# A hybrid encoder layer: gate tiles first, seven products for every q, k and v block, and attention pairs of two groups in turn

## The chip, the cores and the metric

The kernel runs on one core of one Trainium2 chip, in float32: products are built from pairs of rounded float32 (`float32r`) parts, a high and a low one. The metric is device microseconds of one execution; each kernel is timed in several executions, and one execution is profiled. Engines are named as in the profile: PE is TensorE, PEld its weight loads, DVE VectorE, ACT ScalarE, POOL GpSimd, SP SyncE, whose queue issues all the DMAs of this kernel.

## What is computed

The input x has 512 positions (a grid of 8 rows by 64 columns) of 2048 values. One projection gives q, k, v and a gate for two groups of 16 heads of 64 values:

```
h = einsum('bsd,de->bse', x, w_in)                     # 2048 -> 8192
qa, ka, va, ga, qb, kb, vb, gb = split(h)              # 1024 columns each
ya = dilated_attention(qa, ka, va, t5_bias)            # group A, all 512 keys under a mask
yb = neighbourhood_attention(qb, kb, vb, na_rpb)       # group B, 8 rows x 16 columns of keys
y  = concat(ya * silu(ga), yb * silu(gb))
x  = layer_norm(alpha * x + y @ w_out)
```

Group A merges three dilated windows by their softmax denominators, which is one softmax over all keys with a bias that holds mask, bucket bias and multiplicity. Group B has a learned bias by row and column distance.

## The kernel before

**Products in parts.** Every factor is split into a high part (ACT copies it to `float32r`) and a low part (DVE subtracts), `split`, L81 to L83. A product takes three matmuls: high x high, low x high, high x low.

**Stages.** They follow each other on PE:

1. `plain_block` (L219) computes v of group A directly: 16 slices of the contraction, 8 accumulators of 128 x 512 in all eight PSUM banks, three matmuls for each, 384 in all. While it runs, ACT and DVE split x and build the sums of its quarters that the next stage needs (`combine`, L277).
2. `strassen_block` (L292) computes each of the five other q, k and v blocks from quarters, with seven products instead of eight (p1, p5, p7, p6, p3, p2, p4 in this order). A product takes 48 matmuls of 512 columns (v) or 96 of 256 (q, k). Weights come in tiles `braw` of 512 KB; DVE adds two tiles (L332) ahead of four of the products. Results are stored to DRAM by `store_v` and `store_kq`, high and low parts side by side.
3. Between blocks, `prep_a` (L130, after k of group A) builds group A's bias: a small float32 product of 33 rows by 16 columns (L139), 16 row DMAs to `rows_d`, and 8 DMAs that spread them to `biasa_d`. `prep_b` (L147, after q of A and k of B) builds group B's: 17 loads into `rpbs`, three DVE tables `gt`, 24 DMAs to `biasb_d`, rows of 1152.
4. The attention stage (L572 to L597) is one loop of 132 steps; a step is a quarter of a head's queries (128), and 32 heads in pairs make 128. Pairs 0 to 7 are group A, 8 to 15 group B. Step n issues on PE: the scores of step n (two matmuls, L465 and L466 or L473 and L474), the transposes of step n - 3 (L486), at every fourth step the product with v of the head before (L506), and between them fillers (`fill`), which are matmuls of other work. The order of PE in this loop is that of the program. The fillers are first the 16 gate tiles (`gate_unit`, L392, 48 matmuls each, two weight units of 512 KB), then half of the output projection for all four column blocks (`out_first`, L541, 384 matmuls); `amount` (L577) says how many a step takes.
5. A score step goes PE (`sc`), DVE (L437: adds the bias, takes the minimum), ACT (L439: exponent and its sum), DVE (L441: reciprocal), ACT or DVE (scaling), PE (transpose `pt`), ACT (`th`, L492), DVE (`tl`, L493), and after four steps PE with v, then ACT and DVE (L513 to L521) for the gated result `yk`.
6. The rest of the output projection (384 matmuls) and the layer norm.

**Loads of a pair.** `load_pair` (L406) loads one pair ahead: q in two DMAs of 256 KB, high parts on partitions 0 to 63 and low parts on 64 to 127; k in four DMAs of 256 KB, each head's high and low rows on both partition halves; v in four DMAs. The scores multiply the stacked q (128 rows) with k's high part and then with k's low part. Gate results stay in SBUF (`sgs`).

**What sets the order.** Outside the attention loop on PE, a scheduler places the instructions of each engine by its own estimate. ACT, DVE and the queue of SP work strictly in that order; a DMA whose tile is not free yet holds up all DMAs behind it on SP.

Of the kernel before, what the change touches and what calls it, by code (L numbers as in the profile page):

```python
# [12 lines left out]
D = 2048  # L13
# [49 lines left out]
BLOCKS = (("v", 0), ("v", 1), ("k", 0), ("q", 0), ("k", 1), ("q", 1))  # L63


def hybrid_layer(tc, xT, xn, w_in, w_gate, w_out, t5x, brow, rpb, cmask, eye, gain, lbias, out):
    nc = tc.nc
    from contextlib import ExitStack
    with ExitStack() as ctx:
# [38 lines left out]
        def load_split(ring, src, name="w"):  # L108
            raw = ring.next(name + "raw")
            nc.sync.dma_start(raw[:, :1024], src)  # L110
            h, l = halves.next(name + "h", F32R), halves.next(name + "l", F32R)
            split(raw[:, :1024], h, l)
            return h, l
# [12 lines left out]
        bias_d = dram.tile([H, 128, 560], F32, name="biasa_d"), dram.tile([H, 128, 1152], F32, name="biasb_d")  # L126
        kq_d = {(kind, g): dram.tile([PAIRS, 128, 2, S], F32, name=f"{kind}{g}_d") for kind in "kq" for g in range(2)}
        v_d = [dram.tile([S, D], F32, name=f"v{g}_d") for g in range(2)]

        def prep_a():  # L130
            nc.sync.dma_start(ident, eye)
            bt = ring_b.next("bias")
            t5 = bt[0:33, 1024:1040]
            nc.sync.dma_start(bt[0:33, :ROW], brow)
            nc.sync.dma_start(t5, t5x)
            row = ring_b.next("bias")
            for i in range(2):
                ps = bank(pss, "sc")
                nc.tensor.matmul(ps[0:16], t5, bt[0:33, 512 * i:512 * i + 512], start=True, stop=True)  # L139
                nc.scalar.activation(row[0:16, 512 * i:512 * i + 512], ps[0:16], AF.Copy)  # L140
            for c in range(16):
                nc.sync.dma_start(rows_d[:, c], row[0:16, :ROW])
            for r in range(8):
                nc.sync.dma_start(bias_d[0][:, 16 * r:16 * r + 16],
                                  _view(rows_d, 463 - 64 * r, [[16 * ROW, 16], [ROW - 1, 16], [1, 560]]))

        def prep_b(g):  # L147
            b0 = slot("b0", F32, "rpbs")
            r = b0[:, :720].rearrange("p (d j) -> p d j", d=15)
            masks = b0[:, 720:864].rearrange("p (v j) -> p v j", v=3)  # L150
            nc.sync.dma_start(masks, cmask)
            for c in range(16):
                nc.sync.dma_start(r[8 * c:8 * c + 8],
                                  _view(rpb, PADB + 8 * g * RPB - 1 + c * (RPBW - 1), [[RPB, 8], [31, 15], [1, 48]]))
            for v in range(3):
                gt = slot("b1", F32, "gt")[:, :720].rearrange("p (d j) -> p d j", d=15)
                w = 32 if v == 0 else 48
                o = 16 if v == 0 else 0
                nc.vector.tensor_tensor(gt[:, :, 0:w], masks[:, v:v + 1, 0:w].to_broadcast([128, 15, w]),
                                        r[:, :, o:o + w], ALU.subtract)  # L160
                if w < 48:
                    nc.vector.tensor_copy(gt[:, :, w:], masks[:, v:v + 1, w:].to_broadcast([128, 15, 48 - w]))
                gt = gt.rearrange("p d j -> p (d j)")
                for k in range(8):
                    nc.sync.dma_start(_view(bias_d[1], (1024 * g + 16 * k) * 1152 + 384 * v,
                                            [[1152, 16], [128 * 1152, 8], [1, 384]]),
                                      gt[:, 48 * (7 - k):48 * (7 - k) + 384])
# [51 lines left out]
        def plain_block(src, g):  # L219
            ring = Ring("r8", "r9", "t4", "t5", "t6", "t7")  # L220
            sums = Ring("t0", "t1", "t2", "t3")
            accs = [[bank(pacc, "acc") for _ in range(4)],
                    [bank(pss, "sc"), bank(pss, "sc"), bank(pst, "pt"), bank(pst, "pt")]]

            def mms(n, k, w, ch, t):
                h, l = X[k][:, 0, 128 * t:128 * t + 128], X[k][:, 1, 128 * t:128 * t + 128]
                cols = slice(512 * ch, 512 * ch + 512)
                acc = accs[ch][t]
                nc.tensor.matmul(acc, h, w[0][:, cols], start=n == 0, stop=False)  # L229
                nc.tensor.matmul(acc, l, w[0][:, cols], start=False, stop=False)  # L230
                nc.tensor.matmul(acc, h, w[1][:, cols], start=False, stop=n == 15)  # L231

            pending, raws, last = None, [], []
            for i in range(8):
                xr = slot(f"r{i}", F32, "xraw")[:, :1024].rearrange("p (s q) -> p s q", s=2)
                raws.append(xr)
                for s in range(2):
                    k, n = i + 8 * s, 2 * i + s
                    if n == 0:
                        raw = ring.next("wraw")  # L240
                        w = halves.next("wh", F32R), halves.next("wl", F32R)

                        def xpart(c):
                            nc.sync.dma_start(xr[:, 0, c], xT[0][:, c])
                            split(xr[:, 0, c], X[0][:, 0, c], X[0][:, 1, c])
# [5 lines left out]
                        xpart(slice(0, 128))  # L251
                        wpart(slice(0, 512))
                        xpart(slice(128, 512))
                        wpart(slice(512, 1024))
                    else:
                        nc.sync.dma_start(xr[:, s], xT[n])
                        split(xr[:, s], X[k][:, 0], X[k][:, 1])
                        w = load_split(ring, src[n])
                    if n < 14:
                        for ch in range(2):  # L260
                            for t in range(4):
                                mms(n, k, w, ch, t)
# [4 lines left out]
            for ch in (1, 0):  # L267
                for t in range(4):
                    for n, k, w in last:
                        mms(n, k, w, ch, t)  # L270
            for t in range(4):
                store("v", g, 1, t // 2, t % 2, accs[1][t])
            combine(7, raws[7], sums)
            for t in range(4):
                store("v", g, 0, t // 2, t % 2, accs[0][t])
# [16 lines left out]
        def strassen_block(src, kind, g):  # L292
# [9 lines left out]
            def product(i, pool, tiles, pre=None):  # L302
                accs = [bank(pool, "acc") for _ in range(2)]
                for u in range(4):
# [4 lines left out]
                    for t in range(2):  # L309
                        for kk in range(2):  # L310
# [11 lines left out]
                            for n in range(2):  # L322
# [4 lines left out]
                                nc.tensor.matmul(o, l[:, c], ah, start=False, stop=k == 7 and n == 1)  # L327
                return accs
# [58 lines left out]
        units = iter(range(32))  # L387
        raw_ring, sg_ring = Ring("r8", "r9"), Ring(*(f"n{i}" for i in range(6, 12)))
# [3 lines left out]
        def gate_unit():  # L392
# [8 lines left out]
            sg = sg_ring.next("sg")  # L401
            nc.scalar.activation(sg, acc, AF.Tanh, scale=0.5)
            nc.vector.scalar_tensor_tensor(sg, sg, 1.0, acc, op0=ALU.add, op1=ALU.mult)
            sgs.append(sg.rearrange(orders[0], b=4, r=8))

        def load_pair(i):  # L406

            g, j = divmod(i, PAIRS)
            t0 = 4 * (i % 2)
            qt = slot(f"t{t0 + 3}", F32R, "q").rearrange("p (a n) -> p a n", a=2)  # L410
            at = 128 * 2 * S * j
            for s in range(2):
                nc.sync.dma_start(f(qt[64 * s:64 * s + 64]),
                                  _view(kq_d["q", g], at + S * s, [[2 * S, 64], [128 * S, 2], [1, S]]))
            qs = [qt[:, a].rearrange("p (b n) -> p b n", b=4) for a in range(2)]
            ks = []
            for a in range(2):
                kt = slot(f"t{t0 + a}", F32R, f"k{a}")
                for d in range(2):
                    nc.sync.dma_start(f(kt[64 * d:64 * d + 64]),  # L420
                                      _view(kq_d["k", g], at + 128 * S * a, [[2 * S, 64], [1, 2 * S]]))
                ks.append(kt.rearrange("p (s n) -> p s n", s=2))
# [3 lines left out]
            return qs, ks, vv.rearrange("p b (h e) -> p b h e", h=2)  # L426
# [23 lines left out]

        def load_bias(h):
            bias = ring_b.next("bias")
            hg = h % 16
            n = 560 if h < 16 else 1152
            nc.sync.dma_start(bias[:, :n], bias_d[h // 16][hg])
            biases[h] = bias

        def scores(n):

            h, b = divmod(n, 4)  # L460
            qs, ks, _ = loaded[h // 2]
# [267 lines left out]
```

## Time and profile before

| what | value |
|---|---|
| three runs | 1017.04, 1021.34 (median), 1022.0 us |
| the profiled execution | 1018.34 us |
| its span (first to last instruction) | 1016.6 us |
| PE, DVE, ACT busy | 98%, 74%, 51% of the span |
| mean granted clock of PE | 0.992 |
| bytes moved | 189.55 MB, mean 186 GB/s |
| plain block, from its first matmul | 5.1 to 92.8 us |
| v of group B | 92.8 to 168.9 us |
| k and q of both groups | 168.9 to 500.6 us |
| attention with fillers, first score to last product with v | 511.5 to 942.6 us |
| last matmul | 1005.2 us |

A row of the timeline has start, length, engine, line, operation, output and inputs, and in brackets how long the engine had waited and for whom; a matmul also shows the rows and columns of the array that it uses. A row of the waits has total, number and longest. A row of the groups has count, busy time, mean in ns, and the idle time ahead. Matmuls are pipelined: each is shown with its modelled end, so that rows overlap, and the pace is read from start to start.

### The profile page before, as it was taken

How to read it: one execution, taken by the hardware profiler on the slowest of the kernel's cores; microseconds unless marked ns; L12 is line 12 of the kernel's file. 1: busy time of each engine (PE TensorE's matmuls, PEld its weight loads, DVE VectorE, ACT ScalarE, POOL GpSimd, SP SyncE). 2: the span in 40 equal slices, each digit the busy share in tenths (PEclk: the TensorE clock that was granted, in tenths of full speed). 3: DMA queues.
4: the chain of work that ended last, by engine and by line, in shares of the span. 5: the costliest groups of instructions: out<-in, count | busy, mean ns of one | idle time of the engine just before them, and what ended most of it. 6: DMA issues, size and time to landing. Idle time of an engine off the chain costs nothing.

```text
span 1016.6 us, 15728 instructions
## 1 busy us (share of the span) xinstructions
PE 992.3 (98%) x5901; PEld 875.3 (86%) x5901; DVE 753.4 (74%) x1257; ACT 520.2 (51%) x862; POOL 13.3 (1%) x13
## 2 busy tenths in 40 slices
PE   9999999999989999999999999999999899999995
PEld 7888888999989999999978888888888788888884
DVE  8826988887858878888657777777766577666677
ACT  7514444444424534454457777777666555556300
POOL 0000000000000000000000000000000000000022
PEclk9999999999989999999999999999999999999998
DMA  9923356347989889535865665655679997545112
GB/s 343 322 88 127 122 162 239 97 132 248 207 230 268 230 250 309 190 125 144 212 201 147 166 166 147 167 167 159 192 207 262 284 213 210 181 132 182 62 63 103
DMA packets 114675, 189.55 MB, mean 186 GB/s; under 512 B 46087, under 2 KB 70279, under 8 KB 114600
## 3 DMA queue, kind: packets, MB, share of 16 engines
q1 hardware_dynamic: 114600, 188.56, 62.4%
q8 instruction: 46, 0.75, 0.3%
q14 instruction: 29, 0.24, 0.1%
HBM read 148.67 MB, written 44.43 MB: 190 GB/s over the span
## 4 chain that ended last, share of the span: by engine, by line
PE 88%; DMA 5%; DVE 3%; SPq 1%; ACT 1%; issue 1%; POOL 0%; DVEq 0%; ACTq 0%; POOLq 0%
PE acc L398 14%; PE acc L537 14%; PE acc L327 9%; PE acc L325 9%; PE acc L326 9%; PE pv L506 5%; PE pt L486 4%; PE acc L319 3%; PE acc L318 2%; PE acc L320 2%; PE acc L229 1%; PE acc L230 1%; PE acc L231 1%; PE sc L466 1%; PE sc L465 1%; DMA wraw<-in_w_gate 1%
## 5 line engine op out<-in xcount | busy, mean ns | idle before, releaser
L82 ACT ACTIVATE wh<-braw 128x1024 fp32r<-128x1024 f32 x140 | 148.5, 1062 | 205.4 <-PE acc L326 151.4
L83 DVE TENSOR_TENSOR wl<-braw,wh 128x1024 fp32r<-128x1024 f32 x140 | 170.5, 1222 | 51.9 <-ACT wh L82 51.9
L325 PE MATMUL acc<-xk,wh 128*128 128x256 f32 x512 | 143.4, 282 | 1.1 <-ACT wh L82 1.1
L326 PE MATMUL acc<-xk,wh 128*128 128x256 f32 x512 | 143.1, 281 | 0.0
L398 PE MATMUL acc<-xk,wh 128*128 128x512 f32 x512 | 142.6, 402 | 0.0
L327 PE MATMUL acc<-xk,wl 128*128 128x256 f32 x512 | 140.6, 281 | 0.0
L83 DVE TENSOR_TENSOR wl<-wraw,wh 128x1024 fp32r<-128x1024 f32 (+1 forms) x73 | 88.1, 1207 | 46.5 <-ACT wh L82 43.2
L439 ACT ACTIVATE p<-s,mn 128x512 f32<-128x512 f32 (+2 forms) x128 | 82.0, 641 | 59.1 <-DVE mn L437 57.6
L327 PE MATMUL acc<-op,wl 128*128 128x256 f32 x384 | 106.4, 286 | 5.2 <-DVE wl L83 5.2
L325 PE MATMUL acc<-op,wh 128*128 128x256 f32 x384 | 108.4, 285 | 0.0
L326 PE MATMUL acc<-op,wh 128*128 128x256 f32 x384 | 108.4, 285 | 0.0
L537 PE MATMUL acc<-wh,yk 128*128 128x512 f32 x320 | 106.5, 401 | 0.0
L82 ACT ACTIVATE wh<-wraw 128x1024 fp32r<-128x1024 f32 (+1 forms) x73 | 76.4, 1046 | 57.0 <-PE pt L230 16.6
L398 PEld LDWEIGHTS acc<-xk,wh 128*128 128x128 f32 x512 | 91.2, 188 | 15.5
L332 DVE TENSOR_TENSOR braw<-braw 128x1024 f32<-128x1024 f32 x80 | 96.6, 1221 | 6.3 <-DMA braw<-in_w_in 5.6
L325 PEld LDWEIGHTS acc<-xk,wh 128*128 128x128 f32 x512 | 97.3, 190 | 2.4 <-ACT wh L82 1.5
L326 PEld LDWEIGHTS acc<-xk,wh 128*128 128x128 f32 x512 | 97.3, 190 | 0.0
L327 PEld LDWEIGHTS acc<-xk,wl 128*128 128x128 f32 x512 | 95.9, 190 | 0.0
L492 ACT ACTIVATE th<-pt 128x512 fp32r<-128x512 f32 (+2 forms) x128 | 65.5, 513 | 42.2 <-PE pt L486 40.6
L493 DVE TENSOR_TENSOR tl<-pt,th 128x512 fp32r<-128x512 f32 (+2 forms) x128 | 75.0, 587 | 15.2 <-ACT th L492 14.1
L327 PEld LDWEIGHTS acc<-op,wl 128*128 128x128 f32 x384 | 72.9, 194 | 5.8 <-DVE wl L83 5.8
L325 PEld LDWEIGHTS acc<-op,wh 128*128 128x128 f32 x384 | 74.3, 193 | 0.0
(157 smaller groups left out, 1840.1 us busy)
## 6 DMA issues: line engine op xcount, KB each, us to landing
braw<-in_w_in SPq DMA_DIRECT2D x80, 512.0 KB
wraw<-in_w_gate SPq DMA_DIRECT2D x32, 512.0 KB
k<-k_d SPq DMA_DIRECT2D x64, 256.0 KB
wraw<-in_w_out SPq DMA_DIRECT2D x32, 512.0 KB
biasb_d<-gt SPq DMA_DIRECT2D x48, 192.0 KB
bias<-biasb_d SPq DMA_DIRECT2D x16, 576.0 KB
v_d<-vst SPq DMA_DIRECT2D x16, 512.0 KB
k_d<-kst SPq DMA_DIRECT2D x32, 256.0 KB
```

Source lines behind the costliest of these rows:

```text
L82: nc.scalar.activation(hi, raw, AF.Copy)
L83: nc.vector.tensor_tensor(lo, raw, f(hi), ALU.subtract)
L325: nc.tensor.matmul(o, h[:, c], ah, start=k == 0 and n == 0, stop=False)
L326: nc.tensor.matmul(o, h[:, c], al, start=False, stop=False)
L327: nc.tensor.matmul(o, l[:, c], ah, start=False, stop=k == 7 and n == 1)
L332: nc.vector.tensor_tensor(dst[u], dst[u], other[u], ALU.add)
L398: nc.tensor.matmul(acc, w[:, k * 128:k * 128 + 128], X[8 * u + k][:, s], start=u == 0 and n == 0 and k == 0, stop=u == 1 and n == 2 and k ...
L439: nc.scalar.activation(p[:, :n].rearrange("p (b r c) -> p b r c", r=8, c=16), s[:, :n].rearrange(order, r=8, c=16), AF.Exp, bias=mn, scale ...
L492: nc.scalar.activation(th, pt[:, :nch], AF.Copy)
L493: nc.vector.tensor_tensor(tl, pt[:, :nch], f(th), ALU.subtract)
L506: nc.tensor.matmul(pv[:, q0:q1], vv[:, kc, a], src[:, 128 * s:128 * s + q1 - q0], start=m == 0 and n == 0, stop=m == 1 and n == 3)
L537: nc.tensor.matmul(acc, yk[k][:, s, c], w[:, wk], start=first and kk == 0 and n == 0, stop=last and kk == 1 and n == 2)
```

## The change

- **Opening.** `plain_block` now computes six gate tiles (`EARLY`) instead of v of group A: weights `w_early` of 768 columns a slice, gates as the rows of the result, six accumulators, 288 matmuls (the first slice does two tiles in halves). The gated values go to DRAM (`sg_d`).
- **Blocks.** All six q, k, v blocks go through `strassen_block`, v of group A first.
- **Bias tables.** `prep_a` and `prep_b` return lists of steps, and `strassen_block` runs one after each product (`hooks`): A's during v of group B, B's during k of A and k of B. Group B's rows shrink from 1152 to 896 elements.
- **Attention.** Pairs alternate: A, B, A, B (`ORDER`). Ten gate tiles are left as fillers; all gate results go through `sg_d`, and `load_pair` loads one. `amount` is 6.75 fillers a step on average in the first 64 steps and 5.75 after.
- **Scores.** k is loaded once, in four DMAs of 128 KB, with high and low parts on the two partition halves; q's high part twice (two DMAs of 256 KB) and its low part once (256 KB). The first score matmul multiplies the doubled high part of q (128 rows) with both parts of k, the second q's low part with k's high part, on 64 partitions (`me`).

```diff
+ORDER = [(m % 2, m // 2) for m in range(2 * PAIRS)]
+EARLY = 6
+BIAS = ((0, 32), (256, 48), (640, 32))
+BW = 896
...
-        def plain_block(src, g):
+        def plain_block(src):
...
-            accs = [[bank(pacc, "acc") for _ in range(4)],
-                    [bank(pss, "sc"), bank(pss, "sc"), bank(pst, "pt"), bank(pst, "pt")]]
+            accs = [bank(p, "acc") for p in (pacc, pacc, pacc, pacc, pss, pss)]
+            width = 128 * EARLY
...
+            for j in (4, 5, 0, 1, 2, 3):
+                for n, k, w in last:
+                    mms(n, k, w, j)
+                sg = (vst.next("sg"), 512 * (j % 2))
+                o = sg[0][:, sg[1]:sg[1] + 512]
+                silu(o, accs[j])
+                nc.sync.dma_start(sg_d[j], o)
...
+                next(hooks, lambda: None)()
                 return accs
...
-        plain_block(w_in[0:16], 0)
-        for i, (kind, g) in enumerate(BLOCKS[1:], 1):
-            strassen_block(w_in[16 * i:16 * i + 16], kind, g)
-            if i == 2:
-                prep_a()
-            elif i in (3, 4):
-                prep_b(i - 3)
+        plain_block(w_early)
+        hooks = {1: prep_a(), 2: prep_b(0), 4: prep_b(1)}
+        for i, (kind, g) in enumerate(BLOCKS):
+            strassen_block(w_in[16 * i:16 * i + 16], kind, g, iter(hooks.get(i, ())))
...
+            sg = sg_ring.next("sg")
+            nc.sync.dma_start(sg, sg_d[i])
...
+            for d in range(2):
+                nc.sync.dma_start(f(qt[64 * d:64 * d + 64]), _view(kq_d["q", g], at, [[2 * S, 64], [128 * S, 2], [1, S]]))
+                nc.sync.dma_start(f(kt[64 * d:64 * d + 64, 0]), _view(kq_d["k", g], at + S * d, [[2 * S, 64], [1, S]]))
+            nc.sync.dma_start(f(ql), _view(kq_d["q", g], at + S, [[2 * S, 128], [1, S]]))
+            for d in range(2):
+                nc.sync.dma_start(f(kt[64 * d:64 * d + 64, 1]),
+                                  _view(kq_d["k", g], at + 128 * S + S * (1 - d), [[2 * S, 64], [1, S]]))
...
+            me, cols = slice(64 * a, 64 * a + 64), slice(128 * b, 128 * b + 128)
             sc = bank(pss, "sc")
-            if h < 16:
-                nc.tensor.matmul(sc, q, kh, start=True, stop=False)
-                nc.tensor.matmul(sc, q, kl, start=False, stop=True)
...
+            o, ko = sc, (kt[:, a], kt[me, a])
...
+            for k, (m, q) in enumerate(zip(ko, (qt[:, a, cols], ql[me, cols]))):
+                nc.tensor.matmul(o, q, m, start=k == 0, stop=k == 1)
...
-            for _ in range(16):
-                yield from gate_unit()
+            for j in range(EARLY, 2 * PAIRS):
+                yield from gate_unit(j)
...
-                amount = 8 if n < 64 else 9 if n < 88 else 11
+                amount = (7, 6, 7, 7)[n % 4] if n < 64 else (6, 5, 6, 6)[n % 4]
```

The first place is SP's queue at the bias tables. `braw` are weight tiles of the blocks, `rpbs` the rows of group B's bias, `rows_d` and `biasa_d` group A's rows and their spread form, `k_d` and `v_d` stored results. Before, behind the last tile of the third weight quarter of q of group A:

```order
L298 DMA braw<-in_w_in 128x1024
L151 DMA rpbs<-in_cmask 128x144
L153 DMA rpbs<-in_rpb 8x15x48
L142 DMA rows_d<-bias 16x1024 x5
L207 DMA k_d<-kst 256x1x256 x4
L142 DMA rows_d<-bias 16x1024 x11
L153 DMA rpbs<-in_rpb 8x15x48 x2
L144 DMA biasa_d<-rows_d 16x16x560 x8
L153 DMA rpbs<-in_rpb 8x15x48 x5
L298 DMA braw<-in_w_in 128x1024
```

Now, during v of group B:

```order
L330 DMA braw<-in_w_in 128x1024
L216 DMA v_d<-vst 128x1024 x2
L167 DMA rpbs<-in_cmask 128x144
L169 DMA rpbs<-in_rpb 8x15x48
L149 DMA rows_d<-bias 16x1024 x16
L330 DMA braw<-in_w_in 128x1024 x2
L153 DMA biasa_d<-rows_d 16x16x560 x6
L330 DMA braw<-in_w_in 128x1024 x2
L153 DMA biasa_d<-rows_d 16x16x560 x2
L169 DMA rpbs<-in_rpb 8x15x48 x10
L330 DMA braw<-in_w_in 128x1024
```

Before, 33 table DMAs stand between one weight tile and the next; now 18, then 6, then 12.

The second place is PE at the ninth score step, the first of the second pair (`sc` scores, `k` and `q` the pair's tiles, `acc` and `wh` a gate tile and its weights, `pt` a transpose). Before:

```order
L465 MATMUL sc<-k_5409,q 128x512
L466 MATMUL sc<-k_5409,q 128x512
L398 MATMUL acc<-xk_99,wl 128x512
L398 MATMUL acc<-xk_100,wl 128x512
L398 MATMUL acc<-xk_101,wl 128x512
L398 MATMUL acc<-xk_102,wl 128x512
L486 MATMUL pt<-ident,p 128x128 x4
```

Now:

```order
L507 MATMUL sc<-k,q 128x256
L507 MATMUL sc<-k,ql 128x256
L428 MATMUL acc<-xk_106,wh 128x512
L428 MATMUL acc<-xk_107,wh 128x512
L428 MATMUL acc<-xk_100,wh 128x512
L521 MATMUL pt<-ident,p 128x128 x4
```

The second pair is now of group B, with 256 key columns at its first step, three fillers stand ahead of the transposes instead of four, and the second score matmul reads `ql`.

More of the change, by code (lines that the diff above doesn't have):

```diff
@@ L130, in prep_a @@
         def prep_a():
[L131 to L140, printed above, removed]
@@ new lines, in rows @@
+            def rows():
+                nc.sync.dma_start(ident, eye)
+                bt = ring_b.next("bias")
+                t5 = bt[0:33, 1024:1040]
+                nc.sync.dma_start(bt[0:33, :ROW], brow)
+                nc.sync.dma_start(t5, t5x)
+                row = ring_b.next("bias")
+                for i in range(2):
+                    ps = bank(pss, "sc")
+                    nc.tensor.matmul(ps[0:16], t5, bt[0:33, 512 * i:512 * i + 512], start=True, stop=True)
+                    nc.scalar.activation(row[0:16, 512 * i:512 * i + 512], ps[0:16], AF.Copy)
+                for c in range(16):
+                    nc.sync.dma_start(rows_d[:, c], row[0:16, :ROW])
@@ L500, in values @@
         def values(h):
[L501 to L502 removed]
+            g, i, a, _ = head(h)
+            vv = loaded[i][1]
             pv = bank(pst, "pv")
[L504 removed]
+            for m, (src, parts) in enumerate(zip(turned.pop(h), (opening, whole) if g else (full, full))):
                 for n, (kc, q0, q1, s) in enumerate(parts):
@@ L708 @@
         "w_in": wi,
+        "w_early": we,
         "w_gate": wg,
```

208 lines of the change are left out of this document (103 added, 105 removed).

## The prediction

> **What bounds the kernel now.** I read the head of the page first, then the time by stage.
>
> ```profile
> span 1016.6 us, 15728 instructions
> PE 992.3 (98%) x5901; PEld 875.3 (86%) x5901; DVE 753.4 (74%) x1257; ACT 520.2 (51%) x862; POOL 13.3 (1%) x13
> PE   9999999999989999999999999999999899999995
> PEclk9999999999989999999999999999999999999998
> PE 88%; DMA 5%; DVE 3%; SPq 1%; ACT 1%; issue 1%; POOL 0%; DVEq 0%; ACTq 0%; POOLq 0%
> ```
>
> TensorE (PE) is busy for 98% of the span and makes up 88% of the chain that ended last. It dips in two of the 40 slices, at about 280 and 785 us. So the time is the number of matmuls times their pace, plus what PE loses at a few places. Next the busy times in stretches that I cut at the stage borders (the first matmuls of each source line): plain block, v block, the four k and q blocks in three pieces, the first gate tile, group A, group B in three pieces, end of the output projection, tail. Columns: PE, weight loads, VectorE (DVE), ScalarE (ACT), GpSimd, granted clock, DMA share, GB/s.
>
> ```profile
> 5.10:92.80 87.70, 87.70 (x386) 72.62 (x386) 56.56 (x104) 40.25 (x70) 0.00 (x0) 1.00 0.64 233
> 92.80:168.90 76.10, 76.10 (x337) 63.05 (x336) 66.05 (x68) 36.33 (x42) 0.00 (x0) 1.00 0.55 180
> 264.30:320.00 55.70, 50.50 (x403) 49.89 (x402) 38.46 (x41) 19.18 (x21) 0.00 (x0) 0.94 0.85 237
> 320.00:500.60 180.60, 179.49 (x1510) 179.08 (x1509) 148.44 (x159) 82.68 (x95) 0.00 (x0) 1.00 0.72 213
> 500.60:511.50 10.90, 10.90 (x50) 9.01 (x49) 4.71 (x6) 4.68 (x5) 0.00 (x0) 1.00 0.78 209
> 511.50:714.00 202.50, 201.55 (x1004) 166.06 (x1003) 151.72 (x346) 144.32 (x275) 0.00 (x0) 1.00 0.60 165
> 714.00:780.00 66.00, 66.00 (x350) 56.06 (x349) 46.81 (x123) 43.77 (x98) 0.00 (x0) 1.00 0.76 207
> 780.00:803.00 23.00, 19.63 (x99) 16.09 (x98) 10.51 (x31) 9.67 (x25) 0.00 (x0) 0.97 1.02 303
> 803.00:935.00 132.00, 132.00 (x676) 111.73 (x675) 91.36 (x220) 79.04 (x166) 0.00 (x0) 0.99 0.68 192
> ```
>
> A v block by seven products has 7 x 48 = 336 matmuls of 512 columns and takes 76.1 us: 0.2265 us each. A gate tile has 48 and takes 10.9 us: the same pace. PE idles in 264-320 (5.2 us) and in 780-803 (3.4 us), hardly elsewhere. PE's waits say on whom:
>
> ```profile
> PE acc L327 <- DVE wl L83: 5.2, 3, 3.5
> PE pt L486 <- DVE tl L493: 2.7, 3, 1.3
> PE pv L506 <- ACT th L492: 1.7, 1, 1.7
> PE pv L506 <- DVE tl L493: 0.8, 2, 0.4
> ```
>
> **The blocks.** Before, PE does 384 matmuls for v of group A in the plain block, and 16 gate tiles of 48 as fillers. Now the plain block holds six gate tiles (288), v of group A is a block of 336, and ten gate tiles are left as fillers. The gates cost the same at either place; what goes is 384 - 336 = 48 matmuls x 0.2265 = **-10.9 us**. The work that must stay hidden: the opening now lasts 288 x 0.2265 = 65 us instead of 87.7, and DVE, busy for 56.6 us in it, loses a quarter of its weight splits but keeps the input sums, so some 52 us (80%). The v block held PE full (76.10 of 76.10) with DVE at 66.05 of 76.1, 87%, and now two such blocks stand in a row. I cost both at nothing. If the cover fails, PE waits a few times for one split; 3 us is what I allow in the range.
>
> **The bias tables.** Where PE lost its 5.2 us, SyncE's queue (SPq) and DVE show this:
>
> ```profile
> 252.89 2.24 SPq L142 DMA_DIRECT2D rows_d<-bias  x5
> 258.11 6.82 SPq L142 DMA_DIRECT2D rows_d<-bias  x11
> 273.53 7.93 SPq L153 DMA_DIRECT2D rpbs<-in_rpb  x5
> 283.18 0.36 SPq L298 DMA_DIRECT2D braw<-in_w_in  x1
> 288.24 1.23 DVE L332 TENSOR_TENSOR braw<-braw 128x1024 f32<-128x1024 f32 x1 [4.82 <-DMA braw<-in_w_in]
> 295.41 0.66 DVE L159 TENSOR_TENSOR gt<-rpbs 128x480 f32<-128x480 f32 x1 [2.82 <-DMA rpbs<-in_rpb]
> ```
>
> The weight load braw of 283.18 stood in the queue behind the table DMAs, and DVE, which works in order, waited 4.82 us for it with the splits behind it; then 2.82 us for rpbs. At the pace of 320-500 ((180.6 - 1.1)/1510 = 0.1189 us a record) the 403 matmuls of 264-320 would take 47.9 us: the stretch loses 55.7 - 47.9 = 7.8 us, idle and lowered clock together. The change deals the table work out over the products of three blocks. In SP's new order the sixteen rows_d still go in one run, but ahead of weights that are needed a product later, and braw now stand between the table writes. The wait of DVE for rpbs can come again: the table operation is still one instruction in DVE's order. I take 3.0 us, that wait, as what is left: **-4.8 us**. Bounds: all of it gone (-7.8), or as much again at the second place (+4).
>
> **The attention stage.** Matmuls and transposes per head are the same. Without 288 fillers the stage from 511.5 to 935 shrinks from 423.5 to about 358 us, with nearly the same work on the others.
>
> ```profile
> L83 DVE TENSOR_TENSOR wl<-wraw,wh 128x1024 fp32r<-128x1024 f32 x71 | 86.7, 1222 | 46.5 <-ACT wh L82 43.2 <-PE acc L398 2.8
> L403 DVE SCALAR_TENSOR_TENSOR sg<-sg,acc 128x512 f32<-128x512 f32 x16 | 10.9, 683 | 0.4 <-ACT sg L402 0.4
> k<-k_d SPq DMA_DIRECT2D x64, 256.0 KB
> bias<-biasb_d SPq DMA_DIRECT2D x16, 576.0 KB
> ```
>
> DVE: 151.7 + 46.8 + 10.5 + 91.4 = 300.4 us now; 12 splits x 1.222 and 6 x 0.683 leave, 281.6 remain: 79% of 358 instead of 71%. ACT loses work too; even its whole 144.3 + 43.8 + 9.7 + 79.0 = 276.8 us would be 77% of 358. Alternating the groups spreads DVE's heavier A heads, now 151.72 of 202.5 (75%) in one piece, over the whole stage. So no engine overtakes PE, but its waits for tl and th, 2.7 + 1.7 + 0.8 = 5.2 us, will grow: I take half as much again, **+2.6 us**; bounds 0 and the second rival.
>
> DMA: k goes from four loads of 256 KB a pair to 0.5 MB, q from 0.5 to 0.75 MB, group B's bias rows from 1152 to 896 elements; the gates' way through DRAM adds sixteen loads of 256 KB, and ten stores here; 12 weight units of 512 KB leave. In sum 79 MB (GB/s times us of the four stretches) becomes about 74, in 358 us: 206 GB/s instead of 187, below the 303 that 780-803 moved. A new wait on SP: the load of sg waits for the store of its gate tile, with the pair's q, k and v behind it; but tile j is done after 48 x (j - 6) fillers of the loop, 6.75 a step, so at step 7.1 x (j - 6), and loaded at step 8j - 4, 44 steps later at least. Nothing. The stall of 780-803, where the output weights and the residual rows crowd the queue (DMA share 1.02), comes again at step 64 with the same bytes: 0, bounds -3.4 and +3.
>
> **The score matmuls.** The first of each pair is 128 rows as now; the second has ql on 64 partitions, so TensorE goes from a 128-row to a 64-row product and back 128 times. The trace has one place with fewer rows, the table product L139 (33*16):
>
> ```profile
> 249.43 0.28 PE L327 MATMUL acc<-xk,wl 128*128 128x256 f32 x1
> 249.64 1.89 PE L139 MATMUL sc<-bias 33*16 33x512 f32 x4
> 251.46 0.39 PE L325 MATMUL acc<-xk,wh 128*128 128x256 f32 x1
> 251.68 0.28 PE L326 MATMUL acc<-xk,wh 128*128 128x256 f32 x1
> 249.31 0.19 PEld L327 LDWEIGHTS acc<-xk,wl 128*128 128x128 f32 x1
> 249.64 0.11 PEld L139 LDWEIGHTS sc<-bias 33*16 33x16 f32 x2
> 251.46 0.19 PEld L325 LDWEIGHTS acc<-xk,wh 128*128 128x128 f32 x1 [0.85 <-ACT bias L140]
> ```
>
> Going in, the next matmul starts 0.21 us after L327 instead of 0.12, and its weights are loaded no sooner: 0.09 us. Coming out, L325 loads its weights at its own start instead of one matmul ahead, and L326 follows 0.22 us later instead of 0.12: 0.10 us, with some 0.09 ahead of it, but that start is put down to a wait for ACT. So between 0 and 0.19 us a side, 0 to 0.38 us a score pair. L139 differs in more than rows (16 columns, four passes of float32, a wait of its own), the new product keeps all 128 columns, and none of the rows shows 64 by 128. I take 0, keep both ends, and make the upper one a rival.
>
> The Trainium skill, "TensorEngine Tiling (Array Packing)", Tiling Modes, says that changing the tiling mode, not just the tile, drains TensorE, and lists 64 by 128 as a mode of its own. By that rule the sum would be the first rival's; the 0.09 us ahead of L139 agrees with it for 33 by 16.
>
> **Sum.** The profiled execution took 1018.3 us, its span and 1.7 around it. 1018.3 - 10.9 - 4.8 + 2.6 = 1005.2, say **1005 us**. It lies 3 us below the median of the three runs (1021.34) and inside their spread; I forecast on its scale. Its own range: 996 (no table stall, no crowding, no growth of the waits) to 1013 (tables as before, 3 us in the opening).
>
> **Rivals.** *First: the switch of rows costs.* Place: every second score matmul. With 0.09 + 0.10 us on both sides a pair loses 0.38 us, 128 x 0.38 = 48.6 us on PE; the grown waits vanish in that: 1005.2 - 2.6 + 48.6 = **1051 us**, slower. It eats the gain of 13.1 us from 0.10 us a pair on. For it: the only narrower product in the trace shows gaps on both sides. Against: the exit is mixed with a wait, and the form is another. If only the 0.09 us at the entry is real, 11.5 us are lost: 1014 to 1017, no change.
>
> *Second: DVE becomes the bound of the attention stage.* Its work comes in a chain with ACT and PE (score, minimum, exponent, sum, transpose, split), and no attention stretch shows it above 75%. Stuck there, 281.6/0.749 = 376 us instead of 358: 1005.2 - 2.6 + 17.7 = **1020 us**, no change. Against: 87% in the v block.
>
> *Third: the dealing out of the tables changes nothing,* since the order of SP still puts rows_d and rpbs in runs: 4.8 us come back, **1010 us**, still faster.
>
> **Chances.** Forecast 0.41, third rival 0.07: faster 0.48. Second rival 0.07, the half switch 0.05: no change 0.12. First rival 0.40. A measurement of this kernel can tell about 0.5%, 5 us, from no change. Since both signs hold much, the range reaches from the forecast's low end to just above the first rival, 996 to 1055; the forecast's own is 996 to 1013.
>
> **What would show it.** Right: a v block of 76 us after 65 us of opening; no PE wait over 1 us at the tables; the matmul behind each ql product starting 0.23 us after it (group A). Wrong: gaps of 0.1 to 0.2 us around each ql product, which is the first rival; PE's waits for tl above 10 us, the second; DVE waiting for rpbs over 4 us, the third.

## The result, and the profile after

| kernel | median | lowest to highest | ratio to before, 95% interval |
|---|---|---|---|
| before (measured beside it) | 1021.67 us | 1017.04 to 1022.37 | |
| after | 1050.32 us | 1049.83 to 1051.94 | 1.0293, 1.026 to 1.0326 |

The change makes the kernel 2.9% slower. Forecast were 1005 us; the first rival, the switch of rows, had said 1051. The profiled execution of the kernel after took 1049.83 us. The head of its page:

```profile
span 1048.0 us, 15886 instructions
PE 1027.0 (98%) x5859; PEld 858.8 (82%) x5859; DVE 791.9 (76%) x1301; ACT 530.5 (51%) x880; POOL 13.3 (1%) x13
PEclk9999999989999999999999999999999999999998
PE 92%; DMA 3%; DVE 2%; SPq 1%; issue 1%; ACT 0%; POOL 0%; DVEq 0%; POOLq 0%
```

There are 42 matmul records fewer, and yet PE is busy for 34.7 us longer (1027.0 against 992.3). Whatever was lost is booked as work of PE, or as pauses too short for a row of the waits. The busy times by stage say where: opening, v of A, v of B, the k and q blocks, and the attention with the rest of the output projection.

```profile
4.77:70.70 65.93, 65.93 (x296) 54.85 (x295) 50.61 (x102) 36.92 (x70) 0.00 (x0) 1.00 0.72 256
70.70:146.40 75.70, 75.70 (x335) 62.71 (x334) 64.93 (x67) 35.76 (x40) 0.00 (x0) 1.00 0.50 167
146.40:235.30 88.90, 82.51 (x342) 65.13 (x341) 66.04 (x69) 36.49 (x40) 0.00 (x0) 0.96 0.71 217
235.30:557.30 322.00, 320.44 (x2691) 319.74 (x2691) 265.45 (x277) 143.67 (x160) 0.00 (x0) 1.00 0.58 176
557.30:1036.40 479.10, 479.02 (x2194) 355.10 (x2192) 335.65 (x778) 273.93 (x565) 9.48 (x6) 1.00 0.59 172
```

The stretch of before that answers to the last one:

```profile
500.60:1005.20 504.60, 499.35 (x2482) 415.71 (x2480) 355.28 (x796) 295.16 (x584) 9.49 (x6) 1.00 0.61 173
```

It lost 288 fillers, 288 x 0.2265 = 65.2 us, and should take 439.4 us; it takes 479.1. That is **+39.7 us**, in a stretch in which PE counts as busy for 479.02 of 479.10 us while it loads weights for 355.10 only. The two opening stages run at the old pace. The k and q blocks, 331.7 us before (168.9 to 500.6), take 322.0: **-9.7**. The v block of group B takes 88.9 instead of 76.1: **+12.8**. The waits of PE after, complete but for two of 1.3 and 1.1 us in all:

```profile
PE acc L352 <- DVE wl L87: 6.3, 2, 4.0
PE acc L359 <- DVE wl L87: 0.5, 1, 0.5
```

The first row is the v block of B. The waits for tl and th in the attention stage, 5.2 us before, are gone. The timeline of PE at the first score step after (a row with x6 holds six matmuls):

```profile
568.20 0.39 PE L507 MATMUL sc<-k,q 128*128 128x512 f32 x1
568.52 0.50 PE L507 MATMUL sc<-k,ql 64*128 64x512 f32 x1
568.95 1.63 PE L428 MATMUL acc<-xk,wh 128*128 128x512 f32 x6
```

```profile
568.52 0.18 PEld L507 LDWEIGHTS sc<-k,ql 64*128 64x128 f32 x1 [0.35 <-issue]
568.95 1.43 PEld L428 LDWEIGHTS acc<-xk,wh 128*128 128x128 f32 x7 [0.25 <-issue]
```

The 64-row product starts 0.32 us after the 128-row one, not 0.23: +0.09. The next product starts 0.43 us after it: +0.20. The six fillers take 1.63 - 0.39 = 1.24 us for five steps, where the pace gives 5 x 0.2265 = 1.13: +0.11, nearly all of it ahead of the second. Together 0.39 to 0.40 us a pair, some 50 us in 128 pairs. The rows of PEld show what goes with it: at both changes the weights are loaded only when their own matmul starts (568.52 and 568.95), not one matmul ahead. In group B, with 256 columns, the two steps are 0.21 and 0.31 us, where pad128 (below) has 0.12 and 0.12: the price is about the same for the shorter products.

The v block of B, on the queue of SP and on DVE, and the stretch in which the first wait lies:

```profile
183.79 1.40 SPq L330 DMA_DIRECT2D braw<-in_w_in  x2
...
189.36 14.82 SPq L169 DMA_DIRECT2D rpbs<-in_rpb  x10
...
207.56 1.38 SPq L169 DMA_DIRECT2D rpbs<-in_rpb  x2
```

```profile
196.62 1.23 DVE L365 TENSOR_TENSOR braw<-braw 128x1024 f32<-128x1024 f32 x1 [4.26 <-DMA braw<-in_w_in]
...
212.61 0.66 DVE L176 TENSOR_TENSOR gt<-rpbs 128x480 f32<-128x480 f32 x1 [4.60 <-DMA braw<-in_w_in]
```

```profile
184.00:197.00 13.00, 13.00 (x59) 10.78 (x58) 6.88 (x7) 5.30 (x5) 0.00 (x0) 1.00 1.03 320
```

The first wait, 4.26 us, is for weights that were issued at 183.79, ahead of the ten rpbs loads: they were under way for 12.8 us, with the DMA engines full (share 1.03). The second, 4.60 us, is that of the table operation. Its row names a weight load, but the operation reads rpbs and no weights, and the last landing that it waited for (at 212.29) is that of the rpbs load issued at 208.28. So DVE waited once for weights and once for rpbs, as it did before at q of group A, but the weights that it waited for did not stand behind rpbs in SP's order.

### The profile page after: what moved, and what is told of

Same layout as the page of the kernel before. It is cut to its first block, busy times and chain, and to the rows that moved or that the text cites. A ratio compares the mean times of both kernels' runs of the same rounds, so it can differ in the third digit from the quotient of the medians.

```text
span 1048.0 us, 15886 instructions
## 1 busy us (share of the span) xinstructions
PE 1027.0 (98%) x5859; PEld 858.8 (82%) x5859; DVE 791.9 (76%) x1301; ACT 530.5 (51%) x880; POOL 13.3 (1%) x13
## 4 chain that ended last, share of the span: by engine, by line
PE 92%; DMA 3%; DVE 2%; SPq 1%; issue 1%; ACT 0%; POOL 0%; DVEq 0%; POOLq 0%
PE acc L572 16%; PE acc L428 12%; PE acc L359 10%; PE acc L357 10%; PE acc L358 10%; PE sc L507 7%; PE pt L521 5%; PE pv L541 5%; PE acc L352 4%; PE acc L350 4%; PE acc L351 4%; DMA braw<-in_w_in 2%; PE acc L259 2%; PE acc L260 2%; PE acc L261 2%; PE pt L572 1%
## 5 line engine op out<-in xcount | busy, mean ns | idle before, releaser
L86 ACT ACTIVATE wh<-braw 128x1024 fp32r<-128x1024 f32 x168 | 178.0, 1060 | 224.5 <-PE acc L358 144.1
L87 DVE TENSOR_TENSOR wl<-braw,wh 128x1024 fp32r<-128x1024 f32 x168 | 204.2, 1220 | 64.2 <-ACT wh L86 63.9
L365 DVE TENSOR_TENSOR braw<-braw 128x1024 f32<-128x1024 f32 x96 | 115.8, 1218 | 8.7 <-DMA braw<-in_w_in 7.7
L572 PE MATMUL acc<-wh,yk 128*128 128x512 f32 x320 | 113.2, 415 | 0.0
L357 PEld LDWEIGHTS acc<-xk,wh 128*128 128x128 f32 x512 | 97.3, 190 | 1.6 <-ACT wh L86 1.5
L358 PEld LDWEIGHTS acc<-xk,wh 128*128 128x128 f32 x512 | 97.3, 190 | 0.0
L467 DVE CUSTOM_DVE_ANT_0 s<-sc,bias 128x512 f32<-128x512 f32 (+2 forms) x128 | 75.1, 587 | 28.6 <-PE sc L507 27.1
L428 PE MATMUL acc<-xk,wh 128*128 128x512 f32 x320 | 96.6, 415 | 0.0
L87 DVE TENSOR_TENSOR wl<-wraw,wh 128x1024 fp32r<-128x1024 f32 (+3 forms) x61 | 69.1, 1133 | 30.6 <-ACT wh L86 26.7
L86 ACT ACTIVATE wh<-wraw 128x1024 fp32r<-128x1024 f32 (+3 forms) x61 | 60.0, 984 | 40.4 <-PE acc L260 7.8
L358 PEld LDWEIGHTS acc<-op,wh 128*128 128x128 f32 x384 | 73.0, 190 | 0.0
L357 PEld LDWEIGHTS acc<-op,wh 128*128 128x128 f32 x384 | 73.0, 190 | 0.0
```

The source lines that it names most:

```text
L86: nc.scalar.activation(hi, raw, AF.Copy)
L87: nc.vector.tensor_tensor(lo, raw, f(hi), ALU.subtract)
L357: nc.tensor.matmul(o, h[:, c], ah, start=k == 0 and n == 0, stop=False)
L358: nc.tensor.matmul(o, h[:, c], al, start=False, stop=False)
L365: nc.vector.tensor_tensor(dst[u], dst[u], other[u], ALU.add)
L428: nc.tensor.matmul(acc, w[:, k * 128:k * 128 + 128], X[8 * u + k][:, s], start=u == 0 and n == 0 and k == 0, stop=u == 1 and n == 2 and k ...
```

## The experiments

Theory one: TensorE pays for each change between 128 and 64 rows. Theory two: no price on the rows; the attention stage got too dense for the others. Four runs decide this, each timed with before at 1019.68 us.

**pad128: after, with 128 rows in the second score matmul.** The low part of q lies on its 64 partitions, with zeros on the other 64, so that the sum is the same.

```diff
-            ql = slot(f"t{t0 + 3}", F32R, "ql")[:, :S]
+            ql = slot(f"t{t0 + 3}", F32R, "ql").rearrange("p (a n) -> p a n", a=2)
+            for d in range(2):
+                nc.gpsimd.memset(f(ql[64 * d:64 * d + 64, 1 - d]), 0.0)
... (ql is loaded in two DMAs, one a head)
-            o, ko = sc, (kt[:, a], kt[me, a])
+            o, ko = sc, (kt[:, a], kt[:, a])
... (and q's low part is read on all rows)
```

> The changed kernel, but the second score matmul has 128 rows again: q's low part is loaded into a tile whose other 64 partitions are set to zero, and multiplies all of k's rows. Theory one (each change between a 128-row and a 64-row product costs PE about 0.19 us, two changes a score pair, 128 pairs): some 50 us go, 3 to 8 us come back as PE waiting for the split of the transposes, since DVE gets denser: 1002 to 1012 us, about 0.985 of before. Theory two (the denser attention stage itself is slow: DVE and ACT bound it, the row count does nothing): 1035 to 1050 us.

Measured: 1011.39 us, ratio 0.9924 (0.9893 to 0.9954). Its timeline at a score step, with the weight load of the second score product, its stages v of B and attention, its longer waits in the attention (three rows of 0.2 to 0.3 us are left out), and what stood behind the longest:

```profile
575.69 0.39 PE L510 MATMUL sc<-k,q 128*128 128x512 f32 x1
575.92 0.40 PE L510 MATMUL sc<-k,ql 128*128 128x512 f32 x1
576.15 0.85 PE L428 MATMUL acc<-xk,wh 128*128 128x512 f32 x3
```

```profile
575.70 0.19 PEld L510 LDWEIGHTS sc<-k,ql 128*128 128x128 f32 x1
```

```profile
147.30:233.10 85.80, 80.80 (x340) 63.82 (x340) 63.78 (x67) 35.95 (x40) 0.00 (x0) 0.98 0.72 219
556.50:997.90 441.40, 434.59 (x2193) 361.84 (x2191) 332.71 (x778) 272.71 (x565) 24.39 (x34) 0.99 0.66 187
```

```profile
PE pt L524 <- DVE y L552: 3.7, 2, 3.5
PE pt L524 <- ACT p L476: 1.7, 1, 1.7
PE pt L524 <- DVE tl L531: 0.4, 1, 0.4
```

```profile
751.30 1.06 ACT L86 ACTIVATE wh<-wraw 128x1024 fp32r<-128x1024 f32 x1 [4.42 <-DMA wraw<-in_w_out]
```

All starts are 0.23 us apart, ql's weights are loaded one matmul ahead again (575.70), and the stage takes 441.4 us instead of 479.1, with the same matmuls and one row count. The 37.7 us are less than 50, because losses come back that had vanished in the switches: PE idles for 6.8 us (441.40 - 434.59), and from 753.7 to 760.4 us its clock is at 0.50, which costs some 3 us. That is 9.8 of the 12.3 us; the rest is not accounted for. The longest wait, 3.5 us for y, goes back to weights of the output projection that landed late: ACT waited 4.42 us for them, with DVE's work behind it. DVE is busy for 332.71 of 441.40 us, 75%.

**before64: before, with the second score matmul cut to 64 rows.** It leaves out the low part of q times the low part of k; all else is as before.

```diff
-                nc.tensor.matmul(sc, q, kl, start=False, stop=True)
+                nc.tensor.matmul(sc, q[0:64], kl[0:64], start=False, stop=True)
... (group B likewise)
```

> The kernel before with one edit: the second score matmul multiplies only the upper 64 partitions of q (its high part) with k's low part, so it has 64 rows; low x low is left out. Theory one: 128 x 0.39 = 50 us more on PE, less some 6 us of waits that vanish in it: 1056 to 1068 us. Theory two: no change, 1016 to 1023 us.

Measured: 1061.17 us, ratio 1.0396 (1.037 to 1.0423). Its timeline at the first score step:

```profile
512.14 0.39 PE L465 MATMUL sc<-k,q 128*128 128x512 f32 x1
512.46 0.50 PE L466 MATMUL sc<-k,q 64*128 64x512 f32 x1
512.89 1.86 PE L398 MATMUL acc<-xk,wh 128*128 128x512 f32 x7
```

The same steps of 0.32 and 0.43 us, in a kernel with none of the other edits: the rows alone slow it by 41.5 us.

**before64_halves and before64_apart.** Is it a price per narrow matmul or per change? The first does the 64-row product of before64 in two halves of its columns, one behind the other. The second puts a 128-row filler between the halves, and takes one from the step's end.

```diff
...
+                parts = [(sc, q, kh), (sc[:, 0:256], q[0:64], kl[0:64, 0:256]), (sc[:, 256:512], q[0:64], kl[0:64, 256:512])]
+                for i, n_ in enumerate((0, 1, 2)):
+                    nc.tensor.matmul(*parts[n_], start=i == 0, stop=i == 2)
+                    if i == 1:
+                        fill(1)
...
+                amount = (8 if n < 64 else 9 if n < 88 else 11) - (n < 128)
```

(The last three lines are in before64_apart only. Group B's scores are cut the same way.)

> As the run with 64 rows in the kernel before, but the 64-row product is cut into two matmuls of half the columns, one behind the other (the same low x low term left out). If the price is per change of the row count, two changes a pair stay: within 5 us of that run, 1056 to 1072 us. If it is per 64-row matmul, another 50 us: about 1105 us.

> As the run with two halves, but one filler matmul of 128 rows stands between the halves (and each step takes one filler less), so that there are four changes a pair. Per change of the row count: about 50 us more than with the halves together, 1100 to 1115 us. Per 64-row matmul: the same time as with the halves together, within 5 us.

Measured: 1065.9 us (1.0442, 1.0401 to 1.0483) and 1110.12 us (1.0875, 1.0832 to 1.0918). Twice as many narrow matmuls cost 4.7 us, twice as many changes 44.2 us more: 44.2/256 = 0.17 us a change. Theory one holds, theory two falls: the three runs without the changed kernel's other edits pay the price, and pad128, which keeps those edits, doesn't. Two narrow matmuls in a row cost what one costs; three or more in a row were not tried.

**The bias tables: six runs on top of pad128.** One v block takes 76.2 to 76.4 us when nothing disturbs it and one k block 80; pad128 takes 85.8 for v of B. First theory: the weights stand too late in SP's order, behind the table DMAs. (For the rpbs loads, the rows of the changed kernel above already speak against it.)

*pad128_old_places* runs the steps whole, behind the blocks, as before: behind k of A, q of A and k of B (the text on record below names other blocks).

```diff
-        hooks = {1: prep_a(), 2: prep_b(0), 4: prep_b(1)}
+        hooks = {2: prep_a(), 3: prep_b(0), 4: prep_b(1)}
...
-            strassen_block(w_in[16 * i:16 * i + 16], kind, g, iter(hooks.get(i, ())))
+            strassen_block(w_in[16 * i:16 * i + 16], kind, g, iter(()))
+            for step in hooks.get(i, ()):
+                step()
```

> This is the padded version (128-row second score matmul) with the steps of the bias tables at their old places: whole after the blocks q of A, k of A and q of B, none of them between the products of a block. Theory one (the weights' small loads wait in SP's order behind the tables' DMAs, wherever those are issued): the v block of group B falls from 88.9 to 76-78 us, and the stall comes back behind the first q block, where it cost 7.8 us before the change: 1004-1010 us, 2 to 5 us below the padded version's 1011.4. Theory two (the v block of B is long for a reason of its own, such as VectorE's table operations or its weights): it stays at 85-90 us and the time is 1011-1020.

*pad128_pool_queue* issues every table DMA on GpSimd's queue.

```diff
-                    nc.sync.dma_start(r[8 * c:8 * c + 8],
+                    nc.gpsimd.dma_start(r[8 * c:8 * c + 8],
... (and so in every other DMA of the tables)
```

> This is the padded version with every DMA of the bias tables issued on GpSimd's queue, not on SP's; VectorE's table operations stay where they are between the products. Theory one (SP's order): the weights are no longer behind the tables' DMAs, the v block of group B takes 76-80 us instead of 88.9 and the time is 999-1004 us. Theory two (VectorE's order: a table operation that waits for its data holds the weight sums behind it): the v block of B stays within 3 us of 88.9 and the time is 1008-1015 us.

*pad128_one_dma* makes the 16 rpbs loads of a group one.

```diff
-                for c in range(16):
-                    nc.sync.dma_start(r[8 * c:8 * c + 8],
-                                      _view(rpb, PADB + 8 * g * RPB - 1 + c * (RPBW - 1), [[RPB, 8], [31, 15], [1, 48]]))
+                nc.sync.dma_start(r, _view(rpb, PADB + 8 * g * RPB - 1, [[RPBW - 1, 16], [RPB, 8], [31, 15], [1, 48]]))
```

> This is the padded version with the 16 loads of 8 partitions for a group's table made one load of 128 partitions, on SP's queue as before; 30 DMAs fewer. Theory one (the number of small DMAs that SP issues ahead of the weights): the v block of group B takes 77-82 us instead of 88.9 and the time is 1000-1006 us. Theory two (VectorE's order, or the time of the data itself): the v block of B stays within 3 us of 88.9 and the time is 1008-1015 us.

Measured, with before at 1020.04 us: 1010.72 (0.9916, 0.9896 to 0.9936), 1007.76 (0.9893, 0.9868 to 0.9918), 1005.69 (0.9859, 0.9841 to 0.9877). The blocks, old places first (v of B, then q of group A), then v of B of the two others:

```profile
148.20:224.60 76.40, 76.38 (x337) 62.92 (x336) 65.51 (x67) 35.34 (x38) 0.00 (x0) 1.00 0.50 165
307.20:393.30 86.10, 82.77 (x673) 82.21 (x673) 62.60 (x65) 34.26 (x38) 0.00 (x0) 0.96 0.86 224
```

```profile
147.70:233.60 85.90, 81.36 (x341) 64.88 (x340) 65.17 (x67) 36.21 (x40) 27.12 (x49) 0.96 0.72 222
```

```profile
147.30:230.70 83.40, 80.24 (x340) 63.94 (x339) 65.11 (x68) 35.88 (x39) 0.00 (x0) 0.98 0.76 239
```

At the old places v of B falls as theory one said, though the time just misses its 1004 to 1010 us. The loss moves: 9.4 us leave v of B, 6.2 come at q of A (79.9 in pad128, read from first matmul to first matmul) and 2.0 at k of B (82.6 after 80.6). A queue of their own leaves v of B as it was, as theory two said: SP's order alone is not the cause. There ACT, with the weight splits behind it, waits for a result tile whose store has not landed:

```profile
213.23 0.63 ACT L214 ACTIVATE vst<-w 128x512 fp32r<-128x512 f32 x1 [6.81 <-DMA v_d<-vst]
```

One load instead of 16 brings 2.4 us in the block, of about 5 us between the two profiled executions (1011.39 and 1006.41); 83.4 us lies between the two theories. Next theory: the DMA engines are full in these stretches.

*one_dma_later* adds to pad128_one_dma one block of delay.

```diff
-        hooks = {1: prep_a(), 2: prep_b(0), 4: prep_b(1)}
+        hooks = {2: prep_a(), 3: prep_b(0), 4: prep_b(1)}
```

> This is the padded version with one load a table, and with the table steps one block later: still one step behind each product, but in k of A, q of A and k of B instead of v of B, k of A and k of B. Theory one (a block that takes in the tables' traffic finds the 16 DMA engines full, share 1.0, and its weights come late, whichever block it is): v of B falls from 83.6 to 76-78 us, k of A rises from 81.6 to 84-88, the sum of the two stays within 3 us of 165.2, and the time is 1003-1008 us, against 1005.7. Theory two (only the v block has no room for them): both blocks run at 76-81 us and the time is 996-1001.

*one_dma_weights_pool* instead moves the weights to GpSimd's queue.

```diff
-                    nc.sync.dma_start(raw, src[4 * q + u])
+                    nc.gpsimd.dma_start(raw, src[4 * q + u])
```

> This is the padded version with one load a table, and with the 96 weight loads of the v, k and q blocks issued on GpSimd's queue instead of SP's, so that no weight stands behind a table's DMA in an order of issue; the bytes and the engines that carry them stay the same. Theory one (the 16 DMA engines are full, share 1.0, while the tables are moved): the v block of B stays at 81-87 us against 83.6, and the time is 1003-1009 us. Theory two (the weights are issued too late on SP): v of B falls to 76-78 us and the time is 996-1000.

*later_quarter_rows* takes one_dma_later and moves a quarter of group A's rows.

```diff
-                    nc.sync.dma_start(bias_d[0][:, 16 * r:16 * r + 16],
-                                      _view(rows_d, 463 - 64 * r, [[16 * ROW, 16], [ROW - 1, 16], [1, 560]]))
+                    nc.sync.dma_start(bias_d[0][:, 16 * r:16 * r + 16, 0:140],
+                                      _view(rows_d, 463 - 64 * r, [[16 * ROW, 16], [ROW - 1, 16], [1, 140]]))
```

> This is the version with one load a table and the tables one block later, with a quarter of group A's spread rows: the eight DMAs that write them move 140 KB each instead of 560 KB (3.4 MB less in k of A), and the attention reads that quarter four times, so that group A's bias is not the reference's; the number and the order of the transfers that SP issues around them hardly change. Theory one (the 16 DMA engines' time: the bytes that the tables move in the block make its weights late): k of A falls from 86.7 to 79.5-82.5 us, with no wait of TensorE over 1 us in it, and the time is 995-999 us. Theory two (the number and order of the issues, or VectorE's order): k of A stays at 85-88 us and the time is 1000-1004.

Measured: 1001.96 us (0.9822, 0.98 to 0.9845; before 1019.46), 1013.49 (0.9935, 0.9907 to 0.9963) and 1003.12 (0.9828, 0.9806 to 0.9851; before 1021.43). In one_dma_later the loss moves to k of A, as theory one said, and the time is 1 us below its range. In one_dma_weights_pool v of B takes 89.9 us and the whole is slower, which neither theory allowed. later_quarter_rows came out as theory two said. one_dma_later, v of B and k of A, and ten microseconds of it; then the queue and DVE in k of A:

```profile
147.00:223.20 76.20, 76.18 (x336) 62.77 (x336) 65.32 (x67) 35.02 (x38) 0.00 (x0) 1.00 0.51 165
223.20:310.00 86.80, 84.87 (x679) 82.66 (x678) 66.77 (x70) 36.62 (x41) 0.00 (x0) 0.98 0.81 247
...
260.00:270.00 10.00, 10.00 (x85) 10.00 (x84) 3.39 (x3) 4.23 (x4) 0.00 (x0) 1.00 1.02 327
```

```profile
258.64 1.82 SPq L328 DMA_DIRECT2D braw<-in_w_in  x2
...
264.36 11.95 SPq L181 DMA_DIRECT2D biasb_d<-gt  x8
...
271.60 1.23 DVE L363 TENSOR_TENSOR braw<-braw 128x1024 f32<-128x1024 f32 x1 [6.16 <-DMA braw<-in_w_in]
```

The weights of 258.64 were the last ones issued before the wait and landed only at 271.6, while the DMA share stood at 1.02. It is the kind of wait that the changed kernel has at 196.62. In one_dma_weights_pool it is the table operation that waits, for the stores of the table before it, since gt has one buffer:

```profile
209.58 0.91 DVE L174 TENSOR_TENSOR gt<-rpbs 128x720 f32<-128x720 f32 x1 [9.52 <-DMA biasb_d<-gt]
```

PE then stands still for 8.3 us. And later_quarter_rows, with 3.4 MB less to move, still takes 86.0 us for k of A. The share in the same ten microseconds falls to 0.92, DVE waits 2.41 us for weights instead of 6.16, and then 2.77 us for biasb_d<-gt:

```profile
260.00:270.00 10.00, 10.00 (x86) 10.00 (x85) 5.29 (x5) 3.50 (x4) 0.00 (x0) 1.00 0.92 265
```

```profile
265.77 1.23 DVE L363 TENSOR_TENSOR braw<-braw 128x1024 f32<-128x1024 f32 x1 [2.41 <-DMA braw<-in_w_in]
...
270.91 0.91 DVE L174 TENSOR_TENSOR gt<-rpbs 128x720 f32<-128x720 f32 x1 [2.77 <-DMA biasb_d<-gt]
```

No theory of one cause stands: not SP's order (its own queue changed nothing), not the bytes of group A's rows alone (a fall of less than 1 us where at least 4.2 were expected). What is shown is that a loss of 6 to 14 us follows the table steps to whichever block they are dealt to, and that DVE and ACT, which work in order, pass on whichever transfer lands last. How it splits among late weights, stores and the one buffer of gt stays open; two buffers for gt were not tried. The best version, one_dma_later, is 1.8% faster than the kernel before (0.98 to 0.9845), where the change as it stood is 2.9% slower.

## Why the prediction was wrong, step by step

- **48 matmuls less, -10.9: right.** The opening took 65.9 us (65 forecast) and v of A 75.7 (76), with DVE at 50.6 of 65.9 and 64.9 of 75.7: the cover that the prediction named held.
- **The bias tables, -4.8: wrong in size and sign.** Measured are -9.7 in the k and q blocks, +12.8 in v of B and -0.4 in v of A: +2.7 together, inside the bounds of -7.8 and +4. "Braw now stand between the table writes" was so, but the rpbs loads of group B, dealt to k of A, still stand in v of B (189.36). DVE waited there for weights that SP had issued ahead of them (4.26 us) and for rpbs itself (4.60 us, the sign named for the third rival), and the clock was lowered too. The prediction kept 3.0 us for one wait at one place; two waits came, in a block that had been undisturbed. The term was off by 7.5 us; the third rival, tables unchanged, had it best.
- **The growing waits of the attention, +2.6: the size is near, the reason isn't.** Without the switch (pad128) the stage takes 441.4 us against the 439.4 of the same matmuls at before's losses: +2.0. But the waits for tl and th, which were to grow from 5.2 us, fell to 1.0; 3.7 us for y, behind late output weights, and 1.7 us for ACT came in their place. That the sum agrees is luck. In the kernel after itself these waits are hidden in the slower PE.
- **DMA, the load of sg, DVE's share: right where it can be seen.** No wait of PE goes back to sg. The crowding at step 64 came again in pad128, as was said (the 3.5 us above). DVE is at 77% of pad128's attention loop (271.75 of 351.35 us, first score to last product with v), near the 79% of the forecast, and PE is busy for 344.59 us of it: the second rival did not show.
- **The score matmuls, 0: the step that failed.** The prediction had the right rows (L139) and both ends, 0 and 0.38 us a pair, and took the lower, since the rows were of another form and the exit was mixed with a wait. The runs show 0.39 us a pair: 0.09 ahead of the narrow product, 0.20 behind it, 0.10 behind the next one. The reason "keeps all 128 columns" carried no weight: with all 128 columns and only the rows changed, before64 pays it in full. The rule of the Trainium skill ("TensorEngine Tiling (Array Packing)", Tiling Modes) that a change of mode drains TensorE agrees with this; the runs add the price.

The sum by measured terms: 1018.3 - 10.9 + 2.7 + 39.7 = 1049.8 us, the profiled 1049.83; its terms are read from the same two profiles, so that this checks the bookkeeping alone. The first rival hit 1051 with the right mechanism and partly by luck: its tables were 7.5 us too low, and its 48.6 us for the switch came to 39.7 in the stage's time, because losses that before had there vanished in it (5.25 us of idle PE and some 1.5 us of lowered clock; the rest of the 10 us between 50 and 39.7 is not accounted for). The two nearly cancel.

## What to carry to other kernels

A matmul that used 64 rows between neighbours of 128 was dearer here than one of 128: pad it with zeros to the rows of the others (pad128), or put narrow ones side by side (two in a row cost one pair of changes), and count changes, not matmuls. Where the trace shows a price once, in another form, don't put it at nothing: here the price would have been the better forecast, and its absence the rival. Dealing a disturbing step out over a block only moves the loss as long as the engines behind it work in order and wait for the same transfers; look at what lands last after each remedy, since the next one stands right behind it. And check a wait's row against what the operation reads: the row at 212.61 names weights where the operation waited for its table rows.

## What the runs showed of the hardware

A pause of PE can cost more than its row in the waits. In one_dma_later PE paused for 1.93 us in k of A, ran on at full pace for 1.1 us, and then at half pace. First the timeline around the pause, then two equal stretches, during and after the slow part:

```profile
274.02 0.39 PE L357 MATMUL acc<-op,wl 128*128 128x256 f32 x1 [1.93 <-DVE wl L87]
...
274.96 0.28 PE L355 MATMUL acc<-op,wh 128*128 128x256 f32 x1
...
275.23 0.42 PE L357 MATMUL acc<-op,wl 128*128 128x256 f32 x1
...
278.61 0.28 PE L355 MATMUL acc<-op,wh 128*128 128x256 f32 x1
```

```profile
275.10:278.50 3.40, 3.40 (x19) 3.40 (x18) 3.40 (x5) 0.46 (x1) 0.00 (x0) 0.51 0.67 187
279.00:282.40 3.40, 3.40 (x31) 3.40 (x30) 3.40 (x6) 1.79 (x3) 0.00 (x0) 1.00 0.95 372
```

The granted clock is 0.51 for 3.4 us, 19 records instead of 31: some 1.5 us lost on top of the pause. In the v block of B after the change the pause of 4.0 us is followed by a stretch at 0.62:

```profile
214.50:222.50 8.00, 8.00 (x23) 6.32 (x24) 5.89 (x7) 1.58 (x2) 0.00 (x0) 0.62 0.99 369
```

That is 23 records where the next 8 us hold 37: 14 x 0.2265 = 3.2 us. The clock was at 0.50 from 213.8 to 220.6 us, twice the 3.4 us of the other case. In before it was at 0.50 for 3.4 us from 801.5 on, behind a pause of 1.73 us. The pause of 2.3 us ahead of the one of 4.0, and two of 1.2 and 1.3 us in later_quarter_rows, left the clock at full, so the length of the pause alone does not decide it. The Trainium skill, "TensorE: Matmul & The Clock Gate", Part 1, gives the idle array half its clock and warns of pauses above about 3.4 us; the half clock agrees, but here it also came behind 1.93 and 1.73 us.
